# Adding the pooled part and the residual by accumulating transfers from GpSimd's queue

## The chip, the cores and the metric

The kernel runs on one core of one Trainium2 chip. The metric is the device time of one execution in microseconds (us). Three runs of the kernel before gave 2070.76, 2068.88 and 2068.75 us, so the median is 2068.88 us.

Five engines take part. PE is TensorE, which multiplies matrices and writes to PSUM. DVE is VectorE, which does two-operand elementwise work. ACT is ScalarE, which does one-operand work (copies, casts, squares). POOL is GpSimd. SP is SyncE, which here only issues transfers between HBM and the on-chip tiles (DMAs). Each engine runs its own instructions strictly in the order in which they stand in its stream, and a semaphore makes an instruction wait for one of another engine or for a transfer to land.

## What is computed

The block is a macaron layer on a 1024 by 1024 activation: a SwiGLU feed-forward, a token mixer with two branches, a second feed-forward, and a final norm. The change touches the place where the two branches meet and where the mixer's result joins the residual stream:

```python
gate = jax.nn.sigmoid(gates.reshape(b, s, N_BRANCH, D_MODEL) + gate_bias[l])
merged = gate[:, :, 0] * (ret @ w_ret_up[l]) + gate[:, :, 1] * (pool_out @ w_pool_up[l])
h = h + merged @ w_out[l]
h = h + 0.5 * swiglu_ffn(rmsnorm(h, norm_ffn2[l]), ffn2_w_in[l], ffn2_w_out[l])
```

## The kernel before

**Arithmetic.** Every float32 operand is held as a sum of two shorter numbers, hi and lo. ACT makes hi by a cast (L161, or L165 with a gain) and DVE makes lo by a subtraction (L162, or L166 with a gain). A product is then three matmuls of 128 by 128 against 512 columns (L181 to L183). The large products go by a Strassen scheme of seven products in place of eight: `strassen` makes one group, whose output is a pair of 128 by 1024 tiles, cut into four quarters of 128 by 512. A quarter is named by (tile, half): (0, 0), (0, 1), (1, 0), (1, 1).

**The stage of the change** is `merge`. It has two parts of four groups each:

- groups ru0 to ru3 compute `ret @ w_ret_up`. Their pairs become the merged tiles, the operands of the next part (object `mg`).
- groups wo0 to wo3 compute `merged @ w_out`. Their pairs become the new h, the operands of the second feed-forward (object `ffn2`, names n3..., whose first groups are named c...).

Groups run two by two (`two_by_two`): ru0 with ru1, ru2 with ru3, wo0 with wo1, wo2 with wo3. Each of the seven products of a group is a step of 12 matmuls, and the steps of the two groups alternate in the order L11, L12, S2, S3, S1, L22, S4 (`BY_OPERAND`). Quarter (0, 0) is complete after L12, (1, 1) after S1, (1, 0) after L22 and (0, 1) after S4. Each time `evac` is called for the quarter, with the PSUM bank `in0` and, for (1, 1) and (1, 0), a second addend `in1` that ACT had copied out of PSUM earlier (L526, L543).

**What evac does before the change.** In the ru groups, `begin` has SP load the pooled part (`pm`, already gated, in HBM) into the pair's tiles (L1811), 512 KB a tile. `evac` adds `in1` if there is one (L1820), multiplies with the gate `rg` into a small tile h (L1822), and adds h to the quarter (L1823). In the wo groups, `begin` loads the residual `h1` into the pair (L1839), and `evac` adds the bank to the quarter (L1844), and then `in1` if there is one (L1846). All of these run on DVE.

**Who reads the quarters.** Those of ru go to `handed(mg, ...)`: differences on DVE (`sum1` L351, `sum3` and `t2` L343, `t4_` L382), then the split into hi and lo (names mgR, mgT). Those of wo go first to `ffn2.quarter`: SP stores the quarter to HBM (h2, in the trace h<-wo), and ACT squares it for the norm (L283; DVE adds the squares up, L295). After that come a scaling in place on ACT (`r22`, L338), differences (`sum1` L351, and L345 with a gain) and the splits.

**Order.** The program's text gives work with priorities: a step's weights are prepared `LOOK` = 4 steps ahead of its matmuls, the evacuations stand in `soon()` (high priority), and the operand work for later products waits in `flow`, which lets two pieces go after each step. A planner of the framework then lays down each engine's stream from those priorities and from estimated durations. So the stream of an engine is not always the order of the text.

The weights of a group are two raw tiles that SP loads (names like wo1ra, wo1rb). DVE forms the sums S1 to S4 from them (L484, L497, L501, names like wo1S), and the split gives wo1wS and wo1wL, which PE reads.

Of the kernel before, what the change touches and what calls it, by code (L numbers as in the profile page):

```python
# [15 lines left out]
ADD, SUB, MUL = ALU.add, ALU.subtract, ALU.mult  # L16
# [74 lines left out]
def block_kernel(ctx: ExitStack, tc, x, x_tok, x_two, vecs, f1_in, f1_out, w_in, w_v, pool_w, w_ret, w_pool, w_o,  # L91
                 f2_in, f2_out, f2_far, g_row, rope, decay, consts, out, out_tok):
    nc = tc.nc
    mm = nc.tensor.matmul
    tt = nc.vector.tensor_tensor
    stt = nc.vector.scalar_tensor_tensor
    act = nc.scalar.activation
    copy = nc.scalar.copy
# [24 lines left out]
    def tl(name):  # L123
        return sb.tile([P, S], F32, tag="tl", bufs=N_TL, name=name)

    def t4(name):
        return sb.tile([P, S], F32, tag="t4", bufs=N_T4, name=name)

    def c2(name):
        return sb.tile([P, H], F32, tag="c2", bufs=N_C2, name=name)  # L130
# [7 lines left out]

    def load(dst, src):
        nc.sync.dma_start(dst, src)  # L140

    def eights(name):

        return sb.tile([P, 32], F32, tag="ss", bufs=2, name=name)[:, :8]

    def spill(name, n, width=S):
        return [dr.tile([P, width], F32, tag=f"{name}{i}", name=f"{name}{i}") for i in range(n)]

    def half(t, j):
        return t[:, j * H : (j + 1) * H]  # L150
# [56 lines left out]
    neg = cp.tile([P, NV], F32, name="neg")  # L207
    cst = cp.tile([P, NC], F32, name="cst")
    load(vec, vecs)

    warm = cp.tile([P, 1], F32, name="warm")
# [85 lines left out]
    class Next(Norm):  # L297
# [9 lines left out]
        def quarter(self, mt, tokens, tile):  # L307
            src = tile[:, tokens]
            self.tiles[mt, tokens.start // H] = src
            if self.keep is not None:  # L310
                load(self.keep[mt][:, tokens], src)
            self.square(mt, tokens, src)
# [157 lines left out]
    def strassen(nx, wa, wb, name, evac, end, begin=None, shared=(), dest=None):  # L470
# [5 lines left out]
        def blocks():  # L476
            ra, rb = raw(f"{name}ra"), raw(f"{name}rb")
            load(ra, wa)
            load(rb, wb)
            t.update(L11=half(ra, 0), L12=half(ra, 1), L21=half(rb, 0), L22=half(rb, 1))  # L480
# [665 lines left out]
    h1, h2 = spill("h1", KT), spill("h2", KT)  # L1146
# [4 lines left out]
    pm, ret = spill("pm", KT), spill("ret", KT)  # L1151
# [642 lines left out]
    def two_groups(z):  # L1794

        at, gt = (2 * z, 2 * z + 1), {}

        def fetch(which):
            tile, j = which
            gt[which] = tl(f"rg{z}_{tile}{j}")  # L1800
            for n, i in enumerate(at):
                load(half(gt[which], n), half(gates[i + 4 * tile], j))

        def group(n, i):
            pair = [None, None]
            name = f"ru{i}"

            def begin():
                for tile in range(2):
                    pair[tile] = t4(f"{name}{tile}")  # L1810
                    load(pair[tile], pm[i + 4 * tile])  # L1811
                if n == 0:
                    for which in ((0, 0), (1, 1), (1, 0)):
                        fetch(which)

            def evac(which, in0, in1):
                tile, j = which
                dst, h = half(pair[tile], j), c2(f"{name}h{tile}{j}")
                if in1 is not None:
                    tt(h, in0, in1, ADD)  # L1820
                    in0 = h
                tt(h, in0, half(gt[which], n), MUL)  # L1822
                tt(dst, dst, h, ADD)  # L1823
                mg.tiles[i + 4 * tile, j] = dst
                if n == 1 and which == (0, 0):
                    fetch((0, 1))

            return lambda: strassen(up, w_ret[i], w_ret[i + 4], name, evac, none, begin)

        return [group(n, i) for n, i in enumerate(at)]  # L1830

    def out_group(i):
        pair = [None, None]
        name = f"wo{i}"

        def begin():
            for z in range(2):
                pair[z] = t4(f"{name}{z}")
                load(pair[z], h1[i + 4 * z])  # L1839

        def evac(which, in0, in1):
            tile, j = which
            dst = half(pair[tile], j)
            tt(dst, in0, dst, ADD)  # L1844
            if in1 is not None:
                tt(dst, dst, in1, ADD)  # L1846
            flow.add(lambda: ffn2.quarter(i + 4 * tile, slice(j * H, (j + 1) * H), pair[tile]))

        return lambda: strassen(mg, w_o[i], w_o[i + 4], name, evac, none, begin)
# [222 lines left out]
```

## Time and profile before

| what | value |
| --- | --- |
| median of three runs | 2068.88 us |
| the profiled execution's own time | 2069.82 us |
| its span, first to last instruction | 2068.0 us |
| granted TensorE clock, mean | 0.999 |
| matmuls in the span | 10672 |
| DVE instructions | 3262 |
| ACT instructions | 2061 |
| transfers: bytes moved by SP's main queue | 310.64 MB |

How to read it: the span is cut out of one profiled execution, and some 1.8 us lie around it. PE's busy time is modelled and says that matmuls follow one another, not how fast. Where a matmul starts later than the usual pace after the one before it, PE has lost time, and the difference is what the kernel could gain there. A wait is named with its releaser, the instruction that ended it. `L140` is the line of the helper `load`, from which SP issues its transfers. The stage of the change lies between about 1308 us, where ru0's first matmul starts, and 1457 us, where wo3's last one ends.

### The profile page before, as it was taken

The page shows a single profiled execution, that of the slowest core. Times are in us where ns is not written, and L with a number is a line of the kernel's source. Part 1 is how long each engine was busy: PE and PEld are TensorE (multiplying, and loading weights), DVE is VectorE, ACT ScalarE, POOL GpSimd, SP SyncE. Part 2 cuts the span into 40 slices and gives each one's busy share as a digit, 9 for nine tenths or more (in the row PEclk, how much of TensorE's full clock was granted, in tenths as well). Part 3 has the DMA queues.
Part 4 walks back from the last instruction along what each step waited for, and adds up shares of the span by engine and source line. Part 5 has one row for each costly group of instructions (what it writes and reads, how often), then busy time and mean ns, then how long its engine had stood idle before and what let it go on. Part 6 is the DMA issues. An engine that isn't in the chain of part 4 may idle for free.

```text
span 2068.0 us, 29692 instructions
## 1 busy us (share of the span) xinstructions
PE 2045.2 (99%) x10672; PEld 1810.6 (88%) x10672; DVE 1835.5 (89%) x3262; ACT 1091.5 (53%) x2061; POOL 0.2 (0%) x4
## 2 busy tenths in 40 slices
PE   9999999999999999999999999999999999999998
PEld 7888999988888888888888999888789999998887
DVE  8799998997996798999778888999989989899897
ACT  8545444554653535454447753456645545455454
POOL 0000000000000000000000000000000000000000
PEclk9999999999999999999999999999999999999999
DMA  7232424585543333243336576724223242368642
GB/s 257 88 138 77 143 87 143 199 278 190 186 145 100 115 112 131 85 146 120 122 123 237 189 233 235 253 92 159 75 82 138 88 142 87 133 209 268 215 144 101
DMA packets 118819, 313.57 MB, mean 152 GB/s; under 512 B 13200, under 2 KB 17424, under 8 KB 118672
## 3 DMA queue, kind: packets, MB, share of 16 engines
q1 hardware_dynamic: 118096, 310.64, 44.3%
q8 instruction: 83, 1.36, 0.3%
q10 hardware_dynamic: 576, 1.05, 0.1%
q14 instruction: 64, 0.52, 0.1%
HBM read 220.93 MB, written 90.70 MB: 151 GB/s over the span
## 4 chain that ended last, share of the span: by engine, by line
PE 79%; DVE 14%; ACT 3%; issue 2%; DMA 1%; SPq 0%; ACTq 0%; DVEq 0%
PE a_b L181 2%; PE a_b L182 2%; PE a_b L183 2%; PE c_b L181 2%; PE c_b L182 2%; PE c_b L183 2%; PE a_e L181 2%; PE a_e L183 2%; PE a_e L182 2%; PE c_e L183 2%; PE c_e L182 2%; PE c_e L181 2%; PE a_a L182 1%; PE a_a L181 1%; PE a_a L183 1%
## 5 line engine op out<-in xcount | busy, mean ns | idle before, releaser
L182 PE MATMUL c_b<-n3T,c_wS 128*128 128x512 f32 x176 | 66.8, 380 | 0.0
L181 PE MATMUL c_b<-n3T,c_wS 128*128 128x512 f32 x176 | 66.5, 380 | 0.2 <-ACT n3T L161 0.2
L183 PE MATMUL c_b<-n3T,c_wS 128*128 128x512 f32 x176 | 66.7, 379 | 0.0
L181 PE MATMUL a_b<-n1T,a_wS 128*128 128x512 f32 x168 | 63.7, 379 | 0.0
L182 PE MATMUL a_b<-n1T,a_wS 128*128 128x512 f32 x168 | 63.7, 379 | 0.0
L183 PE MATMUL a_b<-n1T,a_wS 128*128 128x512 f32 x168 | 63.7, 379 | 0.0
L181 PE MATMUL a_a<-n1R,a_wL 128*128 128x512 f32 x120 | 45.5, 379 | 0.0
L183 PE MATMUL a_a<-n1R,a_wL 128*128 128x512 f32 x120 | 45.5, 379 | 0.0
L182 PE MATMUL a_a<-n1R,a_wL 128*128 128x512 f32 x120 | 45.5, 379 | 0.0
L182 PE MATMUL c_a<-n3R,c_wL 128*128 128x512 f32 x112 | 42.7, 381 | 1.1 <-DVE n3R L166 1.1
L181 PE MATMUL c_a<-n3R,c_wL 128*128 128x512 f32 x112 | 42.6, 380 | 0.8 <-ACT c_b L521 0.8
L183 PE MATMUL c_a<-n3R,c_wL 128*128 128x512 f32 x112 | 42.5, 379 | 0.0
L181 PEld LDWEIGHTS c_b<-n3T,c_wS 128*128 128x128 f32 x176 | 33.2, 189 | 5.1 <-ACT n3T L161 0.6
L182 PEld LDWEIGHTS c_b<-n3T,c_wS 128*128 128x128 f32 x176 | 33.3, 189 | 4.8 <-DVE n3T L162 0.3
L183 PEld LDWEIGHTS c_b<-n3T,c_wS 128*128 128x128 f32 x176 | 33.3, 189 | 4.7
L183 PEld LDWEIGHTS a_b<-n1T,a_wS 128*128 128x128 f32 x168 | 31.8, 189 | 4.5
L182 PEld LDWEIGHTS a_b<-n1T,a_wS 128*128 128x128 f32 x168 | 31.8, 189 | 4.4
L181 PEld LDWEIGHTS a_b<-n1T,a_wS 128*128 128x128 f32 x168 | 31.8, 189 | 4.3
L162 DVE TENSOR_TENSOR a_wS<-a_S,a_wS 128x512 fp32r<-128x512 f32 x45 | 30.6, 682 | 5.3 <-ACT a_wS L161 5.2
L161 ACT CAST c_wS<-c_S 128x512 fp32r<-128x512 f32 x46 | 27.8, 622 | 11.8 <-DVE c_S L484 7.4
L182 PE MATMUL c_e<-n3T,c_wL 128*128 128x512 f32 x88 | 33.5, 380 | 0.1
L181 PE MATMUL c_e<-n3T,c_wS 128*128 128x512 f32 x88 | 33.5, 380 | 0.0
(3159 smaller groups left out, 8001.9 us busy)
## 6 DMA issues: line engine op xcount, KB each, us to landing
c_ra<-in_f_in SPq DMA_DIRECT2D x22, 512.0 KB, 3.7
c_rb<-in_f_in SPq DMA_DIRECT2D x22, 512.0 KB, 3.7
a_ra<-in_f_in SPq DMA_DIRECT2D x21, 512.0 KB, 3.8
a_rb<-in_f_in SPq DMA_DIRECT2D x21, 512.0 KB, 3.8
t<-au SPq DMA_DIRECT2D x11, 512.0 KB, 3.0
b<-ag SPq DMA_DIRECT2D x11, 512.0 KB, 3.8
r<-au SPq DMA_DIRECT2D x11, 512.0 KB, 3.7
bra<-in_f_out SPq DMA_DIRECT2D x11, 512.0 KB, 5.3
```

Source lines behind the costliest of these rows:

```text
L161: copy(hi, src)
L162: tt(lo, src, hi.bitcast(F32), SUB)
L181: mm(dst, w[0], m[0], start=start, stop=False, skip_group_check=True)
L182: mm(dst, w[0], m[1], start=False, stop=False, skip_group_check=True)
L183: mm(dst, w[1], m[0], start=False, stop=stop, skip_group_check=True)
```

## The change

A new helper `onto` issues a transfer from GpSimd's queue that adds its source in HBM to its destination tile. For 24 of the 32 quarters of the stage the addition of the pooled part or the residual is taken from DVE and done by such a transfer, after the quarter has been written:

- ru0 and ru1: all eight quarters. `begin` loads nothing. `evac` multiplies with the gate straight into the quarter and issues the transfer.
- ru2 and ru3: quarters (0, 0) and (1, 1). The other two of each pair are loaded ahead as halves and added on DVE as before.
- wo0 and wo1: all eight quarters. Where there is an `in1`, DVE writes `in0 + in1` into the quarter; where there is none, ACT copies the bank into it. Then the transfer adds the residual.
- wo2 and wo3: quarters (0, 0) and (1, 1) in that way, and the other two as before.

```diff
+    def onto(dst, src):
+        nc.gpsimd.dma_start(dst, src, accum_op=ADD)
...
             def begin():
                 for tile in range(2):
                     pair[tile] = t4(f"{name}{tile}")
-                    load(pair[tile], pm[i + 4 * tile])
+                    if z:
+                        load(half(pair[tile], 1 - tile), half(pm[i + 4 * tile], 1 - tile))
...
-                dst, h = half(pair[tile], j), c2(f"{name}h{tile}{j}")
+                dst = half(pair[tile], j)
+                h = c2(f"{name}h{tile}{j}") if z and tile != j or in1 is not None else None
                 if in1 is not None:
                     tt(h, in0, in1, ADD)
                     in0 = h
-                tt(h, in0, half(gt[which], n), MUL)
-                tt(dst, dst, h, ADD)
+                if z and tile != j:
+                    tt(h, in0, half(gt[which], n), MUL)
+                    tt(dst, dst, h, ADD)
+                else:
+                    tt(dst, in0, half(gt[which], n), MUL)
+                    onto(dst, half(pm[i + 4 * tile], j))
...
             for z in range(2):
                 pair[z] = t4(f"{name}{z}")
-                load(pair[z], h1[i + 4 * z])
+                if i > 1:
+                    load(half(pair[z], 1 - z), half(h1[i + 4 * z], 1 - z))
...
-            tt(dst, in0, dst, ADD)
-            if in1 is not None:
-                tt(dst, dst, in1, ADD)
+            if i > 1 and tile != j:
+                tt(dst, in0, dst, ADD)
+                if in1 is not None:
+                    tt(dst, dst, in1, ADD)
+            else:
+                if in1 is not None:
+                    tt(dst, in0, in1, ADD)
+                else:
+                    copy(dst, in0)
+                onto(dst, half(h1[i + 4 * tile], j))
```

## The prediction

> **What bounds the kernel now.** I read the page's first and fourth parts, then a table of the stage by stretches, then who PE waited for.
>
> ```profile
> span 2068.0 us, 29692 instructions
> PE 2045.2 (99%) x10672; PEld 1810.6 (88%) x10672; DVE 1835.5 (89%) x3262; ACT 1091.5 (53%) x2061; POOL 0.2 (0%) x4
> PE 79%; DVE 14%; ACT 3%; issue 2%; DMA 1%; SPq 0%; ACTq 0%; DVEq 0%
> ...
> core 0: us, PE busy (x) PEld busy (x) DVE busy (x) ACT busy (x) POOL busy (x), PEclk, DMA share, GB/s
> 1307.80:1344.30 36.50, 36.50 (x171) 31.95 (x170) 33.29 (x55) 14.75 (x27) 0.00 (x0) 1.00 0.66 241
> 1344.30:1380.50 36.20, 36.20 (x169) 31.73 (x168) 36.20 (x61) 18.93 (x35) 0.00 (x0) 1.00 0.28 89
> 1380.50:1419.70 39.20, 36.58 (x167) 30.72 (x166) 38.35 (x64) 24.48 (x43) 0.00 (x0) 1.00 0.49 173
> 1419.70:1460.00 40.30, 40.30 (x188) 35.30 (x187) 40.08 (x66) 25.03 (x43) 0.00 (x0) 1.00 0.32 112
> ...
> PE wo1b L181 <- ACT wo1wS L161: 1.7, 1, 1.7
> PE c_a L182 <- DVE n3R L166: 1.1, 2, 1.0
> PE c_a L181 <- ACT c_b L521: 0.8, 1, 0.8
> PE wo1b L183 <- DVE wo1wS L162: 0.5, 1, 0.5
> PE wo0e L183 <- DVE wo0wS L162: 0.5, 1, 0.5
> ```
>
> The whole is PE's: 99% busy and 79% of the chain. Only where PE waits can this change give anything. In the stage DVE is the engine without air, 36.20 of 36.20 us and then 38.35 of 39.20 and 40.08 of 40.30, while ACT has about 40% free and POOL and half of the transfers' time lie idle. The waits of PE in and just behind the stage end with weights or operands that DVE made, or that ACT made from them. How much that is worth is seen in PE's starts, not in its busy time:
>
> ```profile
> 1390.70 0.38 PE L181 MATMUL wo0b<-mgT,wo0wS 128*128 128x512 f32 x1
> ...
> 1393.08 0.38 PE L183 MATMUL wo0b<-mgT,wo0wS 128*128 128x512 f32 x1
> 1395.12 0.48 PE L181 MATMUL wo1b<-mgT,wo1wS 128*128 128x512 f32 x1 [1.67 <-ACT wo1wS L161]
> ...
> 1402.16 0.38 PE L181 MATMUL wo1e<-mgT,wo1wS 128*128 128x512 f32 x1
> ...
> 1461.51 0.38 PE L183 MATMUL c_a<-n3R,c_wL 128*128 128x512 f32 x1
> 1462.64 0.48 PE L181 MATMUL c_a<-n3R,c_wL 128*128 128x512 f32 x1 [0.75 <-ACT c_b L521]
> ...
> 1469.57 0.38 PE L181 MATMUL c_b<-n3T,c_wS 128*128 128x512 f32 x1
> ```
>
> One step of 12 matmuls runs from 1390.70 to 1393.08 between its first and last start, so the pace is 2.38 / 11 = 0.216 us. From 1393.08 to 1402.16 there are 25 starts, 5.4 us at that pace, and 9.08 us passed: **the first stall costs 3.7 us**. From 1461.51 to 1469.57 there are again 25 starts in 8.06 us: **the second costs 2.7 us**. Some 1.5 us more are scattered up to 1492. So about 8 us can be had, 0.4% of the time, and no more.
>
> **The change part by part.** First what DVE loses.
>
> ```profile
> 1344.28 0.69 DVE L1822 TENSOR_TENSOR ru1h<-ru1b,rg 128x512 f32<-128x512 f32 x1 [0.64 <-PE ru1b L183]
> 1344.89 0.68 DVE L351 TENSOR_TENSOR mgt<-ru 128x512 f32<-128x512 f32 x1
> 1345.49 0.68 DVE L1823 TENSOR_TENSOR ru<-ru,ru1h 128x512 f32<-128x512 f32 x1
> ...
> 1393.74 0.68 DVE L484 TENSOR_TENSOR wo1S<-wo1S,wo1ra 128x512 f32<-128x512 f32 x1
> ...
> 1395.55 0.68 DVE L162 TENSOR_TENSOR wo1wS<-wo1S,wo1wS 128x512 fp32r<-128x512 f32 x1
> ...
> L1823 DVE TENSOR_TENSOR ru<-ru,ru0h x4: 683/690/692, 1321.5 to 1343.0; 128x512 f32<-128x512 f32 x4
> ...
> L1823 DVE TENSOR_TENSOR ru<-ru,ru2h x4: 680/683/684, 1353.9 to 1381.0; 128x512 f32<-128x512 f32 x4
> L1823 DVE TENSOR_TENSOR ru<-ru,ru3h x4: 680/683/686, 1356.3 to 1383.4; 128x512 f32<-128x512 f32 x4
> ...
> L1844 DVE TENSOR_TENSOR wo<-wo0a,wo x1: 683/683/683, 1390.7 to 1390.7; 128x512 f32<-128x512 f32 x1
> L1844 DVE TENSOR_TENSOR wo<-wo1a,wo x1: 680/680/680, 1393.1 to 1393.1; 128x512 f32<-128x512 f32 x1
> ```
>
> An instruction lasts 0.68 us, but the next starts 0.60 us later (1344.89, 1345.49), and 0.60 is its price on a full DVE. Of the 24 additions removed (12 at L1823, 12 at L1844 or L1846), those of ru0 and ru1 up to 1343 lie before DVE's gap at 1344.28, in which it waited for PE: worth nothing. From there to wo1wS at 1395.55 DVE works back to back, and in that run seven fall: the last of ru1, two of the four of ru2, two of ru3, and wo0a and wo1a. 7 x 0.60 = **4.2 us earlier**, more than the 3.7 us that PE lost to these weights, so by itself the first stall closes.
>
> ```profile
> 1422.62 0.69 DVE L295 TENSOR_TENSOR n3ssq<-n3ssq,n3q 128x512 f32<-128x512 f32 x1 [0.22 <-ACT n3q L283]
> ...
> L1844 DVE TENSOR_TENSOR wo<-wo2a,wo x1: 685/685/685, 1430.0 to 1430.0; 128x512 f32<-128x512 f32 x1
> L1844 DVE TENSOR_TENSOR wo<-wo3a,wo x1: 685/685/685, 1432.5 to 1432.5; 128x512 f32<-128x512 f32 x1
> ```
>
> For the second stall I count only what falls after DVE's next gap, at 1422.62: wo2a and wo3a here, and one of the two additions of (1, 1) in wo2 and in wo3. 4 x 0.60 = 2.4 us of the 2.7. The six between 1395 and 1422 give DVE air before that gap; I count them at nothing.
>
> What is added: six copies on ACT, each beside some 40% of free time there. A row of their kind (0.58 us, L521 below) makes 3.5 us, hidden unless ACT stands still, which is the danger below. The transfers: 8 MB came from HBM by SP before, and 8 MB do now, 24 quarters of 256 KB through GpSimd and eight halves through SP, so the traffic is the same, and SP issues eight fewer. POOL is empty (0.00 in each stretch), and one quarter comes every 2.6 us, a step of 12 matmuls, so its queue doesn't build up.
>
> **The unknown is the landing**, the time from the write of a quarter to its sum. No row shows an accumulating transfer. The nearest:
>
> ```profile
> ru<-pm SPq DMA_DIRECT2D x8, 512.0 KB, 6.6
> ...
> rg<-gt SPq DMA_DIRECT2D x15, 256.0 KB, 4.1
> ...
> h<-wo SPq DMA_DIRECT2D x16, 256.0 KB, 2.0
> ```
>
> 2.0 us is a plain store of that size, 4.1 a plain load of it, and 6.6 a load of twice the bytes, which is what a transfer that reads source and destination takes in. I take 5, and keep 2.0 and 6.6 for the range. [...]
>
> Where does somebody stand ready sooner than 5 us? In most places not: the operand work of ru0's quarters comes 10 us and more after all but the last. The first sharp one is sum1, mgt at 1344.89: it reads ru0's (0, 1), whose last addition starts at 1343.0 in the row of ru0h; the multiplication before it, with one instruction between, is done by about 1342.4. With 5 us it lands at 1347.4, so DVE, if its stream keeps that place, stands for 2.5 us (none at 2.0, 4.1 at 6.6) with ru2's weight sums and everything to wo1wS behind it. But the trace shows that the stream isn't the text's order, since sum1 stands between ru1's multiplication and its addition, so the planner may put free work there. I charge half, 1.25 us. SP gains a wait too: its stores h<-wo must await the landing, and behind them on SP stand weight loads of the next groups. Those are prepared four steps ahead, 4 x 2.6 = 10.4 us, which covers 5 or 6.6; I charge nothing, and a few us at the next pair if that cover is gone. Then DVE is 4.2 - 1.25 = 2.95 us earlier, and that is what the first stall gives back. Sum: 2.95 + 2.4 = **5.4 us**. From the profiled execution's 2069.82 that is 2064.4; that execution lies 0.9 us above the median of 2068.88, from which the same sum gives **2063.5 us**.
>
> **Rivals.** (a) *The landing eats the gain.* DVE keeps sum1's place and waits 2.5 to 4.1 us there, and about as long at the same point of the wo part (the difference n3t of the same quarters). The first stall gives 0.1 to 1.7 us and the second at most 1: 2066 to 2069. For it: an in-order engine and no cover if the planner takes the landing for short. Against it: much ready work with earlier priority behind.
>
> (b) *Slower: ACT stands before a bank copy.* This is the place:
>
> ```profile
> 1420.07 0.38 PE L183 MATMUL wo1b<-mgR,wo1wS 128*128 128x512 f32 x1
> ...
> 1425.47 0.38 PE L181 MATMUL wo2a<-mgR,wo2wL 128*128 128x512 f32 x1
> ...
> 1421.84 0.75 ACT L283 ACTIVATE n3q<-wo 128x512 f32<-128x512 f32 x1 [1.66 <-DVE wo L1844]
> ...
> 1424.54 0.58 ACT L521 COPY wo2b<-wo2a 128x512 f32<-128x512 f32 x1
> ```
>
> On ACT the square of wo1's (0, 1) stands ahead of the bank copy L521, which ends at 1425.12, and PE's next step on that bank starts at 1425.47: 0.35 us of air. In the changed kernel the quarter comes by PE's end at 1420.45, a copy of 0.58, then 5 us: 1426.0. Square (0.75) and bank copy (0.58) bring 1427.4, so PE stands about 2 us, 3.6 at 6.6, and not at all below about 3. In the same way the square of wo0's (0, 0), whose addition now starts at 1390.7, can hold the cast of wo1wS and keep the first stall; and if the copy of wo1's (0, 0) is planned behind that square, a second landing follows the first, another 6 us. With 6.6 us and both places kept: 3.6 here, 2 to 6 more in the first stall, less the 2.7 of the second: 2072 to 2076, **2074** in the middle. It decides from a landing of about 5 us, with squares planned as if it were shorter. Against it: the square ended 2.0 us before L521 began, so the planner had other work to put between.
>
> (c) *GpSimd is shut out while DVE runs.* If an issue of POOL's had to wait for a gap of DVE's, DVE would have to stop itself at each difference that reads a last quarter: two in the ru part and two in the wo part, about 5 us each, 20 us, less the 6.6 us of work taken from it and some air: about 10 us, 2079. For it: POOL is at 0.00 in every stretch, so no row shows it at work beside a full DVE. Against it: SP's transfers go on there (28% of the transfers' time in the stretch with DVE at 36.20 of 36.20). [...]
>
> (d) *Both stalls and the scatter close*, with a landing of 2 to 3 us: 2068.9 - 8 = 2061.
>
> **How the numbers follow.** About 0.2%, 4.1 us, is what a measurement here can tell from no change, so faster means below 2064.7 and slower above 2073.0. Forecast (2062 to 2065): 0.43, of which 0.02 lies above the line. (d): 0.09. (a): 0.27. (b): 0.16, of which 0.03 stays below 2073. (c): 0.05. That the work isn't taken off DVE at all can be left out: the additions are gone from its text. Faster 0.41 + 0.09 = 0.50; same 0.02 + 0.27 + 0.03 = 0.32; slower 0.13 + 0.05 = 0.18. The range runs from (d), with nothing lost anywhere, 2060.7, to 2072, where (b) begins; about 0.2 lies outside.
>
> **What would show it.** Right: L1823 four times instead of 16, L1844 and L1846 twelve in all instead of 24, with PE's waits on wo1wS gone and those on c_a under 1 us. The landing is read from the list of issues. Wrong: a gap of DVE before L351 released by a transfer (a); a gap of ACT before L283 released by a transfer, with PE waiting on L521 or L161 behind it (b); POOL's issues starting only in DVE's gaps (c). If the landing is short and PE still waits on the same weights, my reading of DVE's backlog was wrong.

## The result: 2087.4 us, 18 us slower

The changed kernel takes 2087.43 us (median of 5 runs, 2085.62 to 2088.46) against 2069.5 us for the kernel before on the same chip (2068.75 to 2070.76). The ratio is 1.0085, with a 95% interval from 1.0074 to 1.0095. The forecast of 2063.5 us and its range up to 2072.0 were both missed.

Lines of the helpers stand three further down than before: L181 to L183 are now L184 to L186, L351 is L354, L283 is L286, L521 is L524. The transfers are issued at L143. Below are the head of the changed kernel's page, two rows of its list of DMA issues (count, KB each, median us from issue to landing), and who PE waited for between 1300 and 1520 us (sum, times, longest).

```profile
span 2086.1 us, 29726 instructions
PE 2052.0 (98%) x10672; PEld 1815.5 (87%) x10672; DVE 1823.4 (87%) x3238; ACT 1092.9 (52%) x2067; POOL 21.2 (1%) x28
...
ru<-pm POOLq DMA_DIRECT2D x12, 256.0 KB, 5.1
wo<-h POOLq DMA_DIRECT2D x12, 256.0 KB, 4.5
```

```profile
PE wo2a L184 <- ACT wo2b L524: 7.3, 1, 7.3
PE c_a L184 <- ACT c_b L524: 5.2, 1, 5.2
PE ru3a L184 <- ACT ru3b L524: 3.3, 1, 3.3
```

DVE has 24 instructions fewer, as meant, and the waits on wo1wS are gone from the list. In their place stand three long ones, all of one kind: PE waits for ACT's bank copy (L524). That copy takes the first product of a group from one PSUM bank to a second, and only then may PE add its next product to the first bank.

**What the three stops cost.** I add up, over all matmul starts between 1240 and 1700 us that come more than 0.3 us after the one before, what exceeds the usual 0.216 us. That gives 8.4 us for the kernel before and 25.8 us for the changed one. The difference, 17.4 us, is nearly the whole of the 18.1 us by which the two spans differ. The three stops hold 6.4, 9.6 and 7.5 us of it, more than the waits of 3.3, 7.3 and 5.2 us. The rest follows each stop:

```profile
1428.38 0.38 PE L186 MATMUL wo3a<-mgR,wo3wL 128*128 128x512 f32 x1
1436.07 0.80 PE L184 MATMUL wo2a<-mgR,wo2wL 128*128 128x512 f32 x1 [7.31 <-ACT wo2b L524]
1436.65 0.63 PE L185 MATMUL wo2a<-mgR,wo2wL 128*128 128x512 f32 x1
1437.08 0.63 PE L186 MATMUL wo2a<-mgR,wo2wL 128*128 128x512 f32 x1
...
1439.90 0.38 PE L184 MATMUL wo2a<-mgR,wo2wL 128*128 128x512 f32 x1
```

These are PE's instructions after the second stop (start, duration). Until 1439.6 they start 0.43 us apart, twice the usual pace. The table by stretches gives the clock for the first and the second stop (stretch, its length, busy time of PE, PEld, DVE, ACT and POOL with counts, granted clock, DMA share, GB/s):

```profile
1355.00:1361.20 6.20, 5.79 (x14) 4.61 (x15) 5.70 (x11) 2.56 (x5) 0.87 (x1) 0.50 0.07 6
1361.20:1367.00 5.80, 5.80 (x28) 5.08 (x27) 5.18 (x9) 3.35 (x7) 0.86 (x1) 1.00 0.56 88
1436.00:1440.50 4.50, 4.43 (x12) 3.47 (x12) 2.98 (x6) 2.91 (x6) 0.00 (x0) 0.59 0.47 146
```

PE's busy time says nothing here: 5.79 of 6.20 us hold 14 matmuls, and 5.80 of 5.80 hold 28. The granted clock of 0.50 tells the two apart. So of the 23.5 us of the three stops 16.3 us are standing and about 7.2 us are half clock afterwards.

**The first stop, step by step.** First DVE, then ACT, in the changed kernel (start, duration; in brackets the idle time before it and what ended it):

```profile
1341.79 0.69 DVE L1831 TENSOR_TENSOR ru<-ru0b,rg 128x512 f32<-128x512 f32 x1 [0.65 <-PE ru0b L186]
1342.44 0.69 DVE L165 TENSOR_TENSOR ru3wL<-ru3ra,ru3wL 128x512 fp32r<-128x512 f32 x1
1344.38 0.69 DVE L1831 TENSOR_TENSOR ru<-ru1b,rg 128x512 f32<-128x512 f32 x1 [1.25 <-PE ru1b L186]
1350.11 0.69 DVE L354 TENSOR_TENSOR mgt<-ru 128x512 f32<-128x512 f32 x1 [5.04 <-DMA ru<-pm]
1350.72 0.69 DVE L487 TENSOR_TENSOR ru2S<-ru2rb 128x512 f32<-128x512 f32 x1
```

```profile
1344.18 0.86 POOL L143 DMA_DIRECT2D ru<-pm  x1 [1.82 <-issue]
```

```profile
1352.70 0.62 ACT L164 CAST ru2wS<-ru2S 128x512 fp32r<-128x512 f32 x1 [5.16 <-DVE ru2S L487]
1353.22 1.65 ACT L164 CAST mgR<-ru 128x512 fp32r<-128x512 f32 x3
1354.78 0.57 ACT L524 COPY ru3b<-ru3a 128x512 f32<-128x512 f32 x1
```

The quarter (0, 1) of ru0 is written at 1342.48 (1341.79 + 0.69). GpSimd issues its transfer only at 1344.18, it lands 5.84 us later, and the difference mgt begins at 1350.11: 7.6 us after the write, and 5.04 us of them DVE stands. Behind mgt on DVE is the weight sum ru2S. Behind the cast of that sum on ACT is the bank copy of ru3. PE waits for that copy. So a landing that no matmul needs yet stops PE through two engines that take their work in order.

**The second stop** needs only ACT:

```profile
1413.88 0.62 ACT L164 CAST wo2wL<-wo2ra 128x512 fp32r<-128x512 f32 x1 [1.14 <-DMA wo2ra<-in_w_o]
1421.70 0.75 ACT L286 ACTIVATE n3ssq<-wo 128x512 f32<-128x512 f32 x1 [7.21 <-DMA wo<-h]
...
1426.49 0.72 ACT L341 ACTIVATE wo<-wo,vec 128x512 f32<-128x512 f32 x1 [2.76 <-DMA h<-wo]
...
1431.75 0.74 ACT L286 ACTIVATE n3q<-wo 128x512 f32<-128x512 f32 x1 [0.85 <-DMA wo<-h]
...
1434.79 0.74 ACT L286 ACTIVATE n3q<-wo 128x512 f32<-128x512 f32 x1 [1.82 <-DMA wo<-h]
1435.43 0.58 ACT L524 COPY wo2b<-wo2a 128x512 f32<-128x512 f32 x1
```

ACT stands 7.21 us at a square for a landing, 2.76 us at r22 for a store that itself had to wait for a landing, and 0.85 and 1.82 us at two more squares. The bank copy of wo2, whose bank PE had filled by about 1426 (a step of 2.6 us before its last matmul for wo3 at 1428.38), comes last. **The third stop** goes through ACT, DVE and ACT again:

```profile
1466.80 0.75 ACT L286 ACTIVATE n3q<-wo 128x512 f32<-128x512 f32 x1 [5.16 <-DMA wo<-h]
```

```profile
1467.58 0.69 DVE L298 TENSOR_TENSOR n3ssq<-n3ssq,n3q 128x512 f32<-128x512 f32 x1 [2.85 <-ACT n3q L286]
```

A square on ACT waits 5.16 us for a landing. DVE's next addition to the norm waits 2.85 us for that square, and from 1467.58 on DVE runs without a gap to c's weight sum, which ends at 1477.95. ACT casts that sum at 1478.04, and behind the cast stands the copy c_b, at 1479.17. ACT's wait for this weight sum is 3.61 us, as long as in the kernel before; what is new is how late the sum comes for PE, whose last matmul ahead of the stop starts at 1474.27.

### The profile page after: what moved, and what is told of

Its sections match the earlier page's. It is cut to its first block, busy times and chain, and to the rows that moved or that the text cites. A ratio compares the mean times of both kernels' runs of the same rounds, so it can differ in the third digit from the quotient of the medians.

```text
span 2086.1 us, 29726 instructions
## 1 busy us (share of the span) xinstructions
PE 2052.0 (98%) x10672; PEld 1815.5 (87%) x10672; DVE 1823.4 (87%) x3238; ACT 1092.9 (52%) x2067; POOL 21.2 (1%) x28
## 4 chain that ended last, share of the span: by engine, by line
PE 77%; DVE 12%; issue 5%; DMA 3%; ACT 2%; POOL 0%; SPq 0%; ACTq 0%; POOLq 0%; DVEq 0%
PE a_b L184 2%; PE a_b L185 2%; PE a_b L186 2%; PE c_b L184 2%; PE c_b L185 2%; PE c_b L186 2%; PE a_e L184 2%; PE a_e L186 2%; PE a_e L185 2%; PE c_e L186 1%; PE c_e L185 1%; PE c_e L184 1%; PE a_a L186 1%; PE a_a L185 1%; PE a_a L184 1%
## 5 line engine op out<-in xcount | busy, mean ns | idle before, releaser
L186 PE MATMUL c_b<-n3T,c_wS 128*128 128x512 f32 x176 | 66.7, 379 | 0.0
L184 PE MATMUL c_b<-n3T,c_wS 128*128 128x512 f32 x176 | 66.5, 380 | 0.0
L184 PE MATMUL a_b<-n1T,a_wS 128*128 128x512 f32 x168 | 63.7, 379 | 0.0
L186 PE MATMUL a_b<-n1T,a_wS 128*128 128x512 f32 x168 | 63.7, 379 | 0.0
L184 PE MATMUL c_a<-n3R,c_wL 128*128 128x512 f32 x112 | 43.5, 389 | 5.2 <-ACT c_b L524 5.2
L184 PE MATMUL a_a<-n1R,a_wL 128*128 128x512 f32 x120 | 45.5, 379 | 0.0
L186 PE MATMUL a_a<-n1R,a_wL 128*128 128x512 f32 x120 | 45.5, 379 | 0.0
L186 PE MATMUL c_a<-n3R,c_wL 128*128 128x512 f32 x112 | 43.2, 386 | 0.0
L184 PEld LDWEIGHTS c_b<-n3T,c_wS 128*128 128x128 f32 x176 | 33.2, 189 | 4.8 <-ACT n3T L164 0.4
L186 PEld LDWEIGHTS c_b<-n3T,c_wS 128*128 128x128 f32 x176 | 33.3, 189 | 4.7
L186 PEld LDWEIGHTS a_b<-n1T,a_wS 128*128 128x128 f32 x168 | 31.8, 189 | 4.5
L184 PEld LDWEIGHTS a_b<-n1T,a_wS 128*128 128x128 f32 x168 | 31.8, 189 | 4.4
L165 DVE TENSOR_TENSOR c_wS<-c_S,c_wS 128x512 fp32r<-128x512 f32 x46 | 31.9, 695 | 2.6 <-ACT c_wS L164 2.5
```

The costliest lines, as they stand in the source:

```text
L165: tt(lo, src, hi.bitcast(F32), SUB)
L184: mm(dst, w[0], m[0], start=start, stop=False, skip_group_check=True)
L186: mm(dst, w[1], m[0], start=False, stop=stop, skip_group_check=True)
```

## The experiments

**The theory:** DVE and ACT take their work in order and stand for landings; bank copies stand behind them; PE stops, and runs at half clock after a stop. **The rivals:** the transfers themselves cost, by their number, their traffic or the accumulation; GpSimd is shut out by a full DVE; the six copies added on ACT hold the bank copies. "PE lost" is the sum over starts from above, each from the one execution of the run that was profiled; the ratio is to the kernel before in the same session.

| kernel | median, us | ratio to before (95%) | PE lost 1240 to 1700, us |
| --- | --- | --- | --- |
| before | 2069.5 | | 8.4 |
| changed | 2087.4 | 1.0085 (1.0074 to 1.0095) | 25.8 |
| e1: ru part alone | 2074.9 | 1.0027 (1.0017 to 1.0037) | 14.5 |
| e2: wo part alone | 2080.1 | 1.0054 (1.0039 to 1.0069) | 19.2 |
| e3: no transfers | 2065.0 | 0.9980 (0.9971 to 0.9990) | 3.8 |
| e4: plain transfers | 2076.8 | 1.0036 (1.0023 to 1.0049) | 15.2 |
| e5: readers 4 steps later | 2075.1 | 1.0028 (1.0017 to 1.0039) | 14.3 |
| e6: readers 2 steps later | 2082.8 | 1.0065 (1.0051 to 1.0079) | 22.5 |
| e7: before, readers 4 steps later | 2066.7 | 0.9987 (0.9978 to 0.9996) | 6.4 |
| e8: far quarters alone | 2068.7 | 0.9997 (0.9988 to 1.0006) | 8.5 |
| e9: e5, two quarters on DVE | 2075.0 | 1.0023 (1.0013 to 1.0033) | 14.8 |
| e10: ru part alone, readers later | 2067.1 | 0.9993 (0.9984 to 1.0002) | 6.6 |
| e11: far quarters, readers later | 2065.0 | 0.9981 (0.9973 to 0.9990) | 5.7 |
| e12: e5, four quarters on DVE | 2070.6 | 1.0008 (0.9999 to 1.0017) | 8.1 |

### e1 and e2: one part at a time

e1 takes `two_groups` from the changed kernel and `out_group` from the kernel before; e2 the other way round.

> The change in the ru part alone; the wo part is that of the kernel before. Theory (engines that take their work in order stand for the landing, a bank copy stands behind them, and PE's stop costs half clock afterwards): the stop at ru3a stays and costs about 6.6 us, the stop of before at wo1wS (3.7 us) goes, the 2.7 us at c_a stay: 2069.5 + 6.6 - 3.7 = about 2072. Rival (what costs is the number of transfers through GpSimd, or their traffic, wherever they are): half of the loss, 2078. Rival (GpSimd is shut out by a full DVE): as much as in the wo part, 2078.

> The change in the wo part alone; the ru part is that of the kernel before. Theory: no stop at ru3a; the stops at wo2a and c_a stay with 9.9 and 7.8 us; the 2.7 us of before at c_a go, and of the 3.7 us at wo1wS about a third, since two additions of DVE ahead of it went to ACT: 2069.5 + 17.7 - 2.7 - 1.2 = about 2083. Rival (number of transfers or traffic): half of the loss, 2078.

Who PE waited for, first e1 and then e2:

```profile
PE ru3a L184 <- ACT ru3b L524: 4.3, 1, 4.3
```

```profile
PE wo2a L184 <- ACT wo2b L524: 5.0, 1, 5.0
PE c_a L184 <- ACT c_b L524: 4.7, 1, 4.7
```

Each stop stays with the part that was said to make it, and PE's losses add up: 6.1 us over the kernel before in e1 and 10.8 in e2 make 16.9, against 17.4 for both. Both forecasts were 3 us off. In e1 the old stop at wo1wS did not go (3.0 us between 1385 and 1420, 3.7 before): DVE spent its relief standing 6.1 us at mgt. In the changed kernel only 0.3 us are lost there. PE's being held up at ru3a doesn't by itself explain that, since it is held up as much in e1 (6.3 us against 6.4); but in the changed kernel DVE stands 1.1 us less at mgt and is rid of two more additions ahead of wo1wS, and these two were not separated. In e2 the stop at wo2a was 5.0 us where 7.3 were expected. Equal shares by number of transfers, 2078 us for each, don't fit either: the two lie 5.2 us apart, and each stop stands where its own part put it.

### e3: without the transfers

```diff
     def onto(dst, src):
-        nc.gpsimd.dma_start(dst, src, accum_op=ADD)
+        pass
```

This kernel leaves the pooled part and the residual out of the 24 quarters, and moves 6 MB less.

> The changed kernel without the 24 accumulating transfers: the pooled part and the residual are left out of those quarters, and nobody waits for a landing; DVE's relief and ACT's six copies stay. Theory: PE's three stops go, and what is left is the gain that was forecast from DVE's relief alone, 5 to 8 us: 2061 to 2065. Rival (ACT's added copies hold the bank copies): at least one of the stops stays, over 2070. Rival (DVE's relief is worth nothing, and the old stops come back): 2069.

```profile
PE c_b L184 <- ACT n3T L164: 1.9, 1, 1.9
PE c_b L185 <- DVE n3T L165: 0.5, 1, 0.5
```

These are all of PE's waits between 1300 and 1520 us. With the six copies still on ACT no bank copy is late any more, so those copies are not the cause. The kernel is 4.2 us faster than the one before: that is what the relief of DVE is worth when no landing has to be waited for (and 6 MB are not moved, which was not separated). Nothing is lost between 1385 and 1420, so the forecast's seven additions less on DVE did close the first old stall. Between 1455 and 1520 us 3.0 us are still lost, against 4.0 before.

### e4: plain transfers in place of accumulating ones

```diff
-        nc.gpsimd.dma_start(dst, src, accum_op=ADD)
+        nc.gpsimd.dma_start(dst, src)
```

The transfer overwrites the quarter, so this kernel leaves the product out of it.

> The changed kernel with plain transfers in place of accumulating ones, on the same queue at the same places: they overwrite the quarter, so the product is left out of those quarters. Streams and waits are the same. Theory: any landing of 4 us or more brings the same stops; if a plain one lands as late as an accumulating one, 2085 to 2088, and each us by which it lands earlier takes up to 1 us off each of three stops and of the half clock behind it. Rival (the accumulation, which reads the destination as well, is what costs): the landing falls to about 2.6 to 3 us, the stops go, 2062 to 2068.

Two rows of its list of DMA issues, and two of PE's waits:

```profile
ru<-pm POOLq DMA_DIRECT2D x12, 256.0 KB, 3.6
wo<-h POOLq DMA_DIRECT2D x12, 256.0 KB, 3.3
```

```profile
PE wo2a L184 <- ACT wo2b L524: 5.2, 1, 5.2
PE c_a L184 <- ACT c_b L524: 2.5, 1, 2.5
```

The median landing is 1.5 us shorter in the ru part and 1.2 us in the wo part. The 2.6 to 3 us of the rival were an estimate, which neither median shows. With that the stop at ru3a is gone, c_a falls from 5.2 to 2.5 us, and wo2a from 7.3 to 5.2 us. The time lies between the two theories. The accumulation makes landings longer and so counts, but a plain transfer at the same places is still 7.6 us slower than the kernel before.

### e5, e6 and e7: the readers moved back

In e5 and e6 the readers of accumulated quarters go into the text 4 and 2 steps later: the store and square of wo's quarters, the early r22, sum1 and sum3, and r11 of the last two groups. `Flow` counts the steps down and then adds the work. e7 does the same (4 steps) in the kernel before.

```diff
-            flow.add(lambda: ffn2.quarter(...))
+            ffn2.tiles[i + 4 * tile, j] = dst
+            flow.defer(0 if i > 1 and tile != j else LATE, lambda: ffn2.quarter(...))
...
-                    flow.add(*(... for m in (nx.r22, nx.sum1, nx.sum3)))
+                    flow.defer(LATE, *(... for m in (nx.r22, nx.sum1, nx.sum3)))
...
-                flow.add(*(lambda i=i: f[m](i) for i in range(2, 4)))
+                flow.defer(0 if m else LATE, *(lambda m=m, i=i: f[m](i) for i in range(2, 4)))
```

> The changed kernel with the readers of the quarters moved back: the store and the square of an accumulated quarter of wo, the early r22, sum1 and sum3 of the first two groups of each part, and r11 of the last two stand 4 steps (about 10 us) later in the text. All 24 transfers stay. Theory (it is the place of the reader in an in-order stream that costs, not the transfer): the stops at ru3a, wo2a and c_a go or fall under 1.5 us each, 2061 to 2066, as without the transfers. Rival (transfers and their traffic cost): at least 2075. Rival (the postponed squares make the norm late, and c_a waits for that): the first two stops go, the one at c_a stays at 3 us or more, 2068 to 2076.

> The same with 2 steps (about 5 us) in place of 4. Theory: the landing takes 4 to 8 us, so most but not all waits are covered; one of the three stops may be left: 2063 to 2073, not below the one with 4 steps by more than 2 us, unless the norm's lateness (the rival there) decides.

> Control: the kernel before with the same readers moved back by 4 steps, with its additions on DVE and no transfer on GpSimd's queue. Theory: the moving by itself is worth little, 2066 to 2071. Rival (it is the moving that gains): as fast as the changed kernel with the readers moved.

All of PE's waits of 1 us and more in e5, and ACT in e5 ahead of the copy that PE waits for:

```profile
PE wo2a L184 <- ACT wo2b L524: 6.4, 1, 6.4
PE c_b L184 <- ACT n3T L164: 1.6, 1, 1.6
```

```profile
1412.37 0.75 ACT L286 ACTIVATE n3ssq<-wo 128x512 f32<-128x512 f32 x1 [6.70 <-DMA wo<-h]
...
1425.68 0.74 ACT L286 ACTIVATE n3q<-wo 128x512 f32<-128x512 f32 x1 [2.69 <-DMA wo<-h]
1426.33 0.58 ACT L524 COPY wo2b<-wo2a 128x512 f32<-128x512 f32 x1
```

The time, 2075.1 us, misses the 2061 to 2066 of the theory and would fit the rival that the transfers cost. PE's waits decide between them. Two of the three stops (ru3a and c_a) go with all 24 transfers in place, so these two came from the place of the readers. The one at wo2a stays, and ACT's waits ahead of it are in the second fence: though the text names the squares 4 steps later, the planner still lays them ahead of the bank copy. Presumably ACT has free time there by its reckoning; that was not looked into. With 2 steps the stop at ru3a is gone, but those at wo2a (7.6 us) and c_a (3.5 us) are there, with new ones at wo1a (1.6 us) and ru3b (1.3 us): a miss, 2063 to 2073 expected and 2082.8 found.

The control e7 is 2.8 us faster than the kernel before, at the lower edge of what was expected: without any transfer, 1.9 us are lost between 1455 and 1520 us in place of 4.0. Against this control, e5's transfers cost 8.4 us, nearly all of it at wo2a (8.4 us of PE's time between 1420 and 1455).

### e8, e10 and e11: only where the reader is far

e8 uses the transfer in the ru part for all quarters but (0, 1) of ru0 and ru1 and the near ones of ru2 and ru3, and leaves the wo part as it was. e10 is e1, and e11 is e8, with the readers moved back as in e5.

```diff
+            def near(tile, j):
+                return tile != j and (z or j)
...
-                if z and tile != j:
+                if near(tile, j):
```

> The change only where the first reader is far by the trace: in the ru part all quarters but (0, 1) of ru0 and ru1 and (0, 1), (1, 0) of ru2 and ru3; the wo part is that of the kernel before. Against the change in the ru part alone, only two quarters differ. Theory: the stop at ru3a goes; of the 3.7 us at wo1wS the four additions of ru2 and ru3 take 4 x 0.6 = 2.4: about 2066 to 2067. Rival (DVE's wait for the landing isn't what holds ru3a): the stop stays, 2072 or more.

> The change in the ru part alone, all 12 quarters of it, with the readers moved back by 4 steps in both parts; the wo part adds on DVE as before. By PE's starts, the readers moved in the kernel before left 3.7 us lost at wo1wS and 1.9 us behind 1455 us; all ru quarters by transfer with the readers moved left 0.7 us in place of the 3.7. Theory: both together, 2066.7 - 3.0 = 2063 to 2064.5, faster than both kernels. Rival (the stop at ru3a comes back, or the additions of the wo part keep wo1wS late): 2066 or more.

> As the last, but (0, 1) of ru0 and ru1 are added on DVE: the far quarters alone, with the readers moved back by 4 steps. Theory: the far quarters alone left 2.6 us lost at wo1wS in place of 3.7, so 2066.7 - 1.1 = about 2065.5. Rival: nothing gained over the readers moved alone, 2066.7 or more.

e1 and e8 differ in two quarters. In e8 the stop of 4.3 us at ru3a is gone, as the theory says: PE loses nothing between 1300 and 1385. The 2068.7 us are no measurable gain over the kernel before, and 2 us more than expected.

e10 missed its forecast of 2063 to 2064.5 us. A row of DVE's waits in e10 gives a part of why:

```profile
DVE mgt L354 <- DMA ru<-pm: 3.7, 1, 3.7
```

DVE stands 3.7 us for the landing of (0, 1), and the loss at wo1wS is 3.5 us where 0.7 were hoped for. In e11 that quarter is added on DVE, the wait is gone, and 2.2 us are still lost there. So the wait accounts for little more than 1 us. The rest fits the rival, the wo part's additions on DVE: in e5, which has the wo part's transfers, DVE also stands 2.2 us at mgt, and only 0.7 us are lost. e11 came out as forecast (2065.5). It is the only kernel with transfers that is faster than the kernel before by more than its interval, 2065.0 us against 2068.7 in the same session. Most of that is e7's moving of the readers; the intervals of e7 and e11 overlap, so what the ten transfers add to it is not separated.

### e9 and e12: what feeds the stop at wo2a

```diff
e9:
-            if i > 1 and tile != j:
+            if (i > 1 or j) and tile != j:
e12:
-            if i > 1 and tile != j:
+            if tile != j if i > 1 else j:
```

Both are e5 with quarters of wo0 and wo1 added on DVE as before: (0, 1) in e9, (0, 1) and (1, 1) in e12. `begin` (not shown) loads these halves ahead.

> The changed kernel with the readers moved back by 4 steps, and two of the 24 quarters, (0, 1) of wo0 and wo1, added on DVE as before; their squares then wait for DVE and for no landing. Theory (in the run with the readers moved, the stop of 6.4 us at wo2a came from these two squares, which the planner had put ahead of the bank copy of wo2, waiting for the landing; the earlier waits of ACT for landings, 6.7 us at 1405 to 1412 among them, cost PE nothing): the stop goes, and 8 us with it, 2075 - 8 = about 2067, though 20 landings with readers on ACT and DVE stay. Rival (any landing on ACT delays what follows, and the stop only moves): over 2072.

> As the run with the readers moved back and (0, 1) of wo0 and wo1 added on DVE, and (1, 1) of wo0 and wo1 on DVE as well; 20 transfers stay, with the six copies of ACT. In that run the stop at wo2a stayed at 5.0 us, with ACT's 7.1 us wait for the landing of (1, 1) 20 us ahead of it and two more waits, 2.0 and 1.1 us, for the stores behind landings. Theory now (ACT's waits for landings add up along its stream, and the bank copy of wo2 is late by what they leave): without the 7.1 us the stop falls under 1.5 us, with no half clock behind it, 2067 to 2069. Rival (the stop at wo2a comes from DVE, which is late with the two last quarters of wo0 and wo1): it stays at 4 us or more, 2073 to 2076.

ACT in e9, and then in e12:

```profile
1415.94 0.75 ACT L286 ACTIVATE n3ssq<-wo 128x512 f32<-128x512 f32 x1 [7.13 <-DMA wo<-h]
...
1419.92 0.72 ACT L341 ACTIVATE wo<-wo,vec 128x512 f32<-128x512 f32 x1 [1.96 <-DMA h<-wo]
...
1427.98 0.58 ACT L524 COPY wo2b<-wo2a 128x512 f32<-128x512 f32 x1
```

```profile
1419.06 0.75 ACT L286 ACTIVATE n3q<-wo 128x512 f32<-128x512 f32 x1 [4.01 <-DMA wo<-h]
...
1424.17 0.74 ACT L286 ACTIVATE n3q<-wo 128x512 f32<-128x512 f32 x1 [1.15 <-DVE wo L1855]
1424.82 0.58 ACT L524 COPY wo2b<-wo2a 128x512 f32<-128x512 f32 x1
```

I had taken the last two squares ahead of the copy for the cause, and was wrong. In e9 they wait for no landing, and the stop is still 5.0 us. The wait of 7.13 us that ended twelve us earlier had delayed everything behind it. In e12 that wait is gone too, the stop falls to 2.7 us, and no half clock follows it (granted clock 1.00 from 1420 to 1434): 3.2 us are lost between 1420 and 1455, against 8.0 in e9. (The profiled execution of e12 took 2068.7 us, of a range from 2068.2 to 2073.95 us; whether half clock followed the stop in the longer ones is not known.) The direction is the one expected, the sizes (a stop under 1.5 us, 2067 to 2069 us) are not. Another wait of 4.0 us, for the landing of (1, 0), stands in the stream, and the last waits ahead of the copy, 0.72 and 1.15 us, are for DVE's additions; their shares in the 2.7 us were not separated. So it is ACT's waits along its stream, the early ones too, that make the copy late. In the changed kernel those for landings, and for stores behind landings, come to 13.5 us between 1413.88 and 1434.79.

## Why the prediction was wrong, point by point

The step that failed is the charge for the landing: 1.25 us on DVE at sum1, and nothing for ACT, whose case was left to rival (b). The runs showed 5.04 us on DVE, and on ACT 18.4 us at six squares and 3.6 us at two r22. Bank copies stood behind these waits, and PE lost 23.5 us at them. Without landings (e3) none of the three stops is there.

- **What bounds the kernel, and the first stall (3.7 us): right.** e3 closes it with the relief of DVE alone.
- **The second stall (2.4 of 2.7 us to gain): mis-sized.** In e3 only 1.0 us went there, since PE then waits for the cast n3T (1.9 us). The whole relief without a landing is worth 4.2 us in e3, not 6.1, so even a short landing would not have given rival (d)'s 2061 us.
- **ACT's six copies hidden: right** (e3).
- **POOL's queue doesn't build up: nearly.** One quarter every 2.6 us was right, but with three transfers under way GpSimd stood 1.82 and 1.22 us ahead of two issues, and the profile names nothing that ended the wait. One of them was the transfer of the first stop, 1.70 us after its quarter was written.
- **The landing, 5 us between 2.0 and 6.6: the median was right (5.1 and 4.5), the spread was not.** Single ones took 3.8 to 7.95 us from their issue in the changed kernel. The long ones were the ones that mattered: those of the second stop went out at 1413.81 to 1416.94, just behind four weight loads of 512 KB that SP had issued from 1410.26 to 1412.06. The 2 to 3 us of rival (d) were an estimate that no accumulating transfer of the changed kernel shows: the shortest landing there is 3.84 us, and the medians of the plain ones in e4 are 3.6 and 3.3 us.
- **The wait at sum1, charged 1.25 us: wrong.** The stream kept its place, and the wait was 5.04 us. Rival (a) foresaw the wait but only as a loss of the gain; the row behind it, a bank copy on ACT, made it a stop of PE.
- **SP's stores, charged nothing: incomplete.** No stop of PE ended with a weight load, as the prediction said. But r22 on ACT overwrites the quarter that the store reads, so the store's lateness came back on ACT, 2.76 us in the second stop.
- **Rival (b), 2074 us at a chance of 0.16, was the right mechanism at the right place**, the square ahead of wo2's bank copy. **What failed is the reason against it**, which kept the charge for ACT at nothing: "the square ended 2.0 us before L521 began, so the planner had other work to put between". The planner had none that counted: even with the squares named 4 steps later (e5) it laid them ahead of the copy. The same step hides in "In most places not", where the forecast asked who stands ready sooner than 5 us: six squares and two r22 of the wo part did.
- **Rival (b)'s size was short for three reasons**: its wait of PE was 7.3 us instead of 2 to 3.6, because waits of several readers add up; the third stop, at c_a, comes from a square that waits for a landing too, by way of DVE, and was not seen; and the half clock behind the stops, about 7.2 us, was in no sum.
- **Rival (c), GpSimd shut out by DVE: not what happened.** Its issues took 0.86 to 0.89 us at 23 of the 24 places (1.00 us at the first), and without the transfers' landings (e3) or with other readers (e8) the stops at ru3a went.

## What to carry to other kernels

In this kernel an addition that is moved from an engine to an accumulating transfer frees 0.6 us of the engine and adds 4 to 8 us before anyone may read the result (3.84 to 7.95 us from issue to landing in the changed kernel); count who reads each result next on each in-order engine, and what stands behind that reader, above all a copy after which PE may go on in a bank. Use it only for results whose first reader is far, and check in the streams, not in the text, that the reader really stands there. A few us of slack of an engine that is 40% idle on average say nothing about the one place where it stands still.

## What the runs showed of the hardware

Issue of one transfer of 256 KB on GpSimd, first accumulating (changed kernel), then plain (e4):

```profile
1359.25 0.87 POOL L143 DMA_DIRECT2D ru<-pm  x1 [12.11 <-DVE ru L1831]
```

```profile
1353.80 0.54 POOL L143 DMA_DIRECT2D ru<-pm  x1 [9.46 <-DVE ru L1831]
```

The accumulating issue took 0.87 us of GpSimd, the plain one 0.54. The accumulating one landed 4.09 us after its issue, with a DMA share of 0.43 in that time. The six longest landings of the changed kernel come from two places with more traffic: the transfers issued at 1336.53, 1338.91 and 1341.49 took 7.39, 7.04 and 6.67 us (share 0.91 between 1336 and 1353 us), and the three from 1413.81 to 1416.94 took 7.54 to 7.95 us (share 0.90 between 1410 and 1422 us). But the one issued at 1433.37 took 4.15 us with a share of 0.95 in that time. What other transfers cost a landing was not measured by itself.

In the trace of the changed kernel the granted clock is 0.50 for 6.83 us at each of the three stops of PE (3.3, 7.3 and 5.2 us), from 1354.39, 1432.90 and 1477.27 us, and 1.00 for 71.68 and 37.55 us between them. PE was idle for 2.28, 3.41 and 2.62 us of the 3.41 us ahead of each. Behind the stop of 4.3 us in e1 the clock is 0.76 between 1355 and 1362 us, and behind that of 6.4 us in e5 0.55 between 1426 and 1431. Shorter stops went both ways. The clock stays at 1.00 behind the 2.7 us of e12 and the 1.7 us of the kernel before; it is 0.50 behind 2.5 us in e4 (c_a) and 0.55 behind 1.6 us in e5 (between 1478.9 and 1482.0). Here are two stretches of 3.41 us each for e4 and e12, with the columns of the table by stretches above:

```profile
1464.91:1468.32 3.41, 0.91 (x5) 0.48 (x4) 3.41 (x6) 2.18 (x4) 0.00 (x0) 1.00 0.20 77
1468.32:1471.73 3.41, 3.41 (x10) 2.52 (x9) 3.41 (x7) 3.41 (x7) 0.00 (x0) 0.50 0.00 0
```

```profile
1421.37:1424.78 3.41, 1.41 (x7) 0.90 (x5) 3.41 (x7) 1.86 (x3) 0.00 (x0) 1.00 0.30 117
1424.78:1428.20 3.42, 2.75 (x12) 2.19 (x12) 3.42 (x6) 3.42 (x7) 0.00 (x0) 1.00 0.44 105
```

In e4 PE is idle for 2.50 us of one stretch (3.41 - 0.91), and the next has half clock. In e12 it is idle for 2.00 us of one stretch and 0.67 us of the next, and the clock stays at 1.00. What decides between the two, and why half clock stands behind 1.6 us in e5, was not shown.

In the changed kernel none of the 24 issues of GpSimd began with three transfers under way. Those that followed the 1.82 and 1.22 us of standing began 0.25 and 0.31 us after the oldest of the three had landed (at 1343.93 and 1345.95). Whether GpSimd stood for that landing was not tried.
